# A decoder layer on one core: the products of two stages take PSUM banks of several kinds in turn

## The chip, the core and the metric

The kernel runs on one core of a Trainium2 chip. The core has a matrix engine (TensorE, PE in the profile), two engines that work element by element (VectorE, DVE; ScalarE, ACT), a small general one (GpSimd, POOL) and a queue that starts transfers (SyncE, SP). A product of TensorE lands in PSUM, which this kernel uses as eight banks of 128 x 512 float32; VectorE or ScalarE reads it from there. The metric is the device time of one execution in microseconds (us).

## The reference, cut to what matters

One layer for 1024 tokens of width 1024, in float32:

```python
u = rms_norm(h, norm1_g)
aq, ak, av, hq, hf, hi, hg = split(u @ w_in)
attn = rms_norm(dilated_attention(aq, ak, av), attn_norm_g)       # 8 heads
rec = rms_norm(hgrn2_mixer(hq, hf, hi, lb), hgrn_norm_g) * silu(hg)  # 4 heads, chunks of 64
h = h + concat([attn, rec]) @ w_out
u = rms_norm(h, norm2_g)
gate, val = split(u @ w_up)                                       # 2 x 2816 columns
h = h + (gelu(causal_conv3(gate)) * val) @ w_down
return rms_norm(h, final_norm_g)
```

In `hgrn2_mixer` a state of 128 x 128 per head is carried from chunk to chunk; inside a chunk there are products of queries with keys, of the masked result with the values, and of the queries with the state.

## The kernel before

All data lie transposed, features on the 128 partitions and tokens in two halves (`hf`) of 512 columns. Each float32 product is made as three passes: an operand is split into a rounded part (`hi`) and the rest (`lo`), and a block of 512 columns costs `hi*hi`, `hi*lo` and `lo*hi` for each block of 128 rows (`three`, L491 to L493; in the up stage `prod`, L1239 to L1241). The weights come by DMA into a ring of five slots, where ScalarE makes `whi` (L89) and VectorE `wlo` (L91).

The program runs in stages, one after the other on TensorE:

1. Token products, the first query/key blocks, then attention with the remaining query/key blocks between its parts (to 266 us in the profile).
2. The recurrent stage (266 to 389 us). The generator `dense` yields dense products: four blocks for pairs of head projections (`hg_block`, which is `pair_block`: seven products each, combined by additions, in the manner of Strassen), then `plain_block` with four plain products (`phf`, `phq`). Between them `play` sets in the steps of the recurrence, eight chains `recur(h, hf)`, by a table of times: transposes of the keys (`psK`), scores (`psA`), state updates (`psU`), outputs (`psO`), a transpose of the outputs (`psT`). Two sums for the attention's norm (`ass`) come in too.
3. The out-projection (389 to 493 us): `out_block`, 32 products `po`, with the rest of the recurrence and the norm of the first half between them (`norm2(0)`).
4. The up stage begins with six plain products for columns 0 and 1 (`p0g`, `p0v`, `p1g` ...), with `norm2(1)` between the first two: its sum `ss2_1` is two TensorE passes over the parts `acchi` and `acclo` of the accumulated squares. Then 20 blocks of seven products each (`up`), from another pool of eight PSUM banks.
5. The down stage and the final norm.

TensorE's order is the program's own. On the other engines a scheduler sets the order.

Up to the end of stage 4's plain products, `bank(tag, name)` hands out PSUM. There are four kinds (tags) of bank, `mm`, `o`, `t` and `s`, two banks each, and each kind hands out its two in turn: a tile has to wait until the tile two before it in its own kind has been read. The dense products and the out-projection take `mm` alone, the recurrence `s` (`psA`, `psU`), `t` (`psK`, `psT`, also `ass` and `ss2`) and `o` (`psO`). For the last ten products of the out-projection the kinds are already `mm`, `mm`, `s`, `o` in turn, before and after the change.

Of the seven products of a `pair_block`, most are read by one VectorE instruction; the product 5 is read by two (L528 and L529), with other VectorE work between them.

Of the kernel before, what the change touches and what calls it, by code (L numbers as in the profile page):

```python
# [251 lines left out]
def hybrid_kernel(ctx: ExitStack, tc: tile.TileContext, xT, w_qk, w_tok, w_hg, w_out, w_up,  # L252
# [134 lines left out]
    def bank(tag, name):  # L387
        return ps1.tile([P, H2], F32, tag=tag, name=name, bufs=2)
# [13 lines left out]
    def mtile(name):  # L402
        return at.tile([P, H2], F32, tag="m", name=name, bufs=3)
# [51 lines left out]
    def rms1_row(hf):  # L455
        ss = bank("s", f"ss{hf}")
        PE.matmul(ss, ones, sums[hf], start=True, stop=True)
        rstd(R1[:, halves[hf]], xp.tile([P, H2], F32, tag="sq", name=f"rt{hf}", bufs=2), ss, 1.0 / DM)
# [39 lines left out]
    def product(ps, key, i):  # L498

        x, op = TERMS[i]  # L500
        hi, lo = ring.get((key, x))
        bh, bl = opn[op]
        for c in range(KS):
            s = slice(c * P, (c + 1) * P)
            three(ps, (hi[:, s], lo[:, s]), (bh[:, c], bl[:, c]), c == 0, c == KS - 1)
            if c == KS - 1:
                ring.done((key, x))
            yield 0.65

    def pair_block(key, tiles, evac):  # L510

        def step(i):
            blocks.append(i)
            ps = bank("mm", f"w{len(blocks)}")
            yield from product(ps, key, i)
            return ps

        c1 = tiles(0, 0)
        ACT.copy(c1, (yield from step(1)))
        u = tiles(0, 1)  # L520
        DVE.tensor_sub(u, c1, (yield from step(6)))
        DVE.tensor_add(c1, (yield from step(2)), c1)
        evac(0, 0, c1)
        w = tiles(1, 0)
        DVE.tensor_add(w, (yield from step(7)), u)
        x = tiles(1, 1)
        p5 = yield from step(5)
        DVE.tensor_sub(x, p5, w)  # L528
        DVE.tensor_sub(u, u, p5)  # L529
        evac(1, 1, x)  # L530
        DVE.tensor_sub(w, (yield from step(4)), w)
        evac(1, 0, w)
        DVE.tensor_add(u, (yield from step(3)), u)
        evac(0, 1, u)

    blocks = []

    def tok_step(key, c, banks, order):

# [13 lines left out]
    def plain_product(ps, key, hf):  # L553

        for c in range(NCT):
            hi, lo = ring.get((key, c // KS))
            s = slice(c % KS * P, (c % KS + 1) * P)
            bh, bl = opn[OPS1[2 * hf + c // KS]]
            three(ps, (hi[:, s], lo[:, s]), (bh[:, c % KS], bl[:, c % KS]), c == 0, c == NCT - 1)
            if hf and c % KS == KS - 1:  # L560
                ring.done((key, c // KS))
            yield 0.65
# [62 lines left out]
    def run(g):  # L625
        for _ in g:
            pass
# [9 lines left out]
    def qk_evac(p):  # L637
        def evac(m, hf, src):
            if p not in qk:
                qk[p] = [at.tile([P, SEQ], F32, tag=x, name=f"{x}{p}", bufs=2) for x in ("qp", "kp")]  # L640
            t = halves[hf]
            nat = [x.rearrange("p (b l r) -> p b l r", l=32, r=4) for x in (src, R1[:, t])]
            DVE.tensor_mul(qk[p][m][:, t].rearrange("p (b r l) -> p b l r", l=32, r=4), *nat)
        return evac

    def qk_block(p):
        return pair_block(("qk", p), lambda m, hf: mtile(f"u{p}_{m}{hf}"), qk_evac(p))

    FAR, NEAR = 192, 256
    mask = at.tile([P, FAR + NEAR], F32, name="mask")  # L650
    first = qk_block(0)
    for _ in range(KS + 1):
        next(first)
    for hf in range(2):
        rms1_row(hf)
    run(first)
    fill.add(*[qk_block(p) for p in range(1, 4)])
    fill.run(3.9)
    xp_cm.__exit__(None, None, None)
# [164 lines left out]
    with pool("hg", "right") as hg:  # L824
# [8 lines left out]
        def tile_of(kind, h, hf):  # L833
            tag, bufs = {"hf": ("A", 4), "hq": ("E", 5), "hg": ("GH"[h // 2], 4)}[kind]
            return ht(tag, f"{tag}{h}_{hf}", bufs)
# [35 lines left out]
        def hg_block(pair):  # L871

            def evac(m, hf, src):
                DVE.tensor_mul(src, src, R1[:, halves[hf]])
                OUT[pair[m][0]](pair[m][1], hf, src)

            return pair_block(pair, lambda m, hf: tile_of(*pair[m], hf), evac)

        def plain_block(pair):

            for hf in range(2):
                for kind, h in pair:
                    ps = bank("mm", f"p{kind}{h}_{hf}")
                    yield from plain_product(ps, (kind, h), hf)
                    x = tile_of(kind, h, hf)
                    DVE.tensor_mul(x, ps, R1[:, halves[hf]])
                    OUT[kind](h, hf, x)

        def restore():

            for c in range(KS):
                hi, lo = (y[:, c] for y in opn["T4"])
                x = ring.raw(xT[c, :, halves[1]])
                ACT.mul(hi, x, col(V_G1 + c))
                DVE.scalar_tensor_tensor(lo, x, col(V_G1 + c), f32(hi), op0=ALU.mult, op1=ALU.subtract)

        def dense():

            for pair in HG[1:-1]:
                yield from hg_block(pair)  # L900
            restore()
            yield from plain_block(HG[-1])
# [159 lines left out]

        fill.add(dense())
        N = 3.5 * (len(HG) - 2) + 4.0
        steps = []
# [67 lines left out]
            if part:  # L1135
                square(hf, d)

        out_banks = cycle(("mm",))

        def square(hf, d):  # L1140
            t = halves[hf]
# [30 lines left out]
    def norm2(hf):  # L1172
        t = halves[hf]
        ss = bank("t", f"ss2_{hf}")
        sum_parts(ss, accs[hf])
        yield
        if hf:
            y, tt = otile("cv", "r2y_1", 2), otile("w", "r2t_1", 1)
        else:
            y, tt = (n2p.tile([P, H2], F32, name=f"r2{x}_0") for x in "yt")  # L1180
        R = rstd_part(y, tt, ss, 1.0 / DM)
        for c in range(NCT):
            if hf:
                uf = uf1[c] = atile(f"uf2_1_{c}")
            else:
                uf = n2p.tile([P, H2], F32, tag="uf", name=f"uf2_0_{c}", bufs=2)
            DVE.scalar_tensor_tensor(uf, h_[:, c, t], col(V_G2 + c), R, op0=ALU.mult, op1=ALU.mult)
            hi, lo = u2[hf][c]
            ACT.copy(hi, uf)
            DVE.tensor_sub(lo, uf, f32(hi))  # L1190
        yield
# [9 lines left out]
    out_banks = cycle(("mm", "mm", "s", "o"))  # L1201
# [43 lines left out]
    def plain(f, which, hf, last, ps):  # L1245
        for i, x in enumerate(("a11", "a12") if which == "g" else ("a21", "a22")):
            prod(ps, (x, f), u2[hf][i * KS : (i + 1) * KS], i == 0, i == 1, last)
# [70 lines left out]


    n2 = norm2(1)  # L1320
    p0 = {"g": bank("mm", "p0g"), "v": bank("mm", "p0v")}
    plain(0, "g", 0, False, p0["g"])
    next(n2)
    next(n2)
# [33 lines left out]
    with pool("ps2", "left", space=PSUM) as ps2:  # L1358

        def bank2(name):  # L1360
            return ps2.tile([P, H2], F32, tag="u", name=name, bufs=8)
# [159 lines left out]
        for x, y in STAGES:  # L1521
# [10 lines left out]
            ps = [bank2(f"d{x}_{d}") for d in range(KS)]  # L1532
# [107 lines left out]
```

## Time and profile before

| | us |
|---|---|
| median of 3 runs | 1146.88 |
| lowest and highest run | 1146.65, 1148.97 |
| the profiled execution | 1147.14 |
| its span, first to last instruction | 1145.4 |

The profile is of one execution. A row of its timeline gives the start in us, the duration, the engine, the line of the kernel, the operation, and output <- inputs by the program's names with their numbers left out; what stands in brackets is how long the engine was idle before it and what released it. A matmul's duration overlaps with that of the next one: what counts for TensorE is the distance from start to start. The view by windows gives the busy time of each engine in a stretch of time, and in the column PEclk the granted clock of TensorE as a share of full speed.

### The profile page before, as it was taken

How to read it: one execution, taken by the hardware profiler on the slowest of the kernel's cores; microseconds unless marked ns; L12 is line 12 of the kernel's file. 1: busy time of each engine (PE TensorE's matmuls, PEld its weight loads, DVE VectorE, ACT ScalarE, POOL GpSimd, SP SyncE). 2: the span in 40 equal slices, each digit the busy share in tenths (PEclk: the TensorE clock that was granted, in tenths of full speed). 3: DMA queues.
4: the chain of work that ended last, by engine and by line, in shares of the span. 5: the costliest groups of instructions: out<-in, count | busy, mean ns of one | idle time of the engine just before them, and what ended most of it. 6: DMA issues, size and time to landing. Idle time of an engine off the chain costs nothing.

```text
span 1145.4 us, 17931 instructions
## 1 busy us (share of the span) xinstructions
PE 1131.1 (99%) x6416; PEld 928.9 (81%) x6416; DVE 959.7 (84%) x1748; ACT 586.6 (51%) x1177; POOL 88.2 (8%) x107
## 2 busy tenths in 40 slices
PE   9999999999999999999999999999999999999996
PEld 7887777778888888878788888888888888888885
DVE  7676877778999975889999989888988789857987
ACT  6544445465787875555433434343434354444553
POOL 5200233330000002000000000000000000000000
PEclk9999999999999999999999999999999999999998
DMA  7135221224313543221233223322332376335432
GB/s 250 59 99 152 64 76 58 84 75 161 116 59 102 174 129 101 84 65 46 74 111 117 87 100 129 111 82 95 126 111 83 117 267 230 116 98 175 157 120 74
DMA packets 98633, 129.84 MB, mean 113 GB/s; under 512 B 25008, under 2 KB 44240, under 8 KB 98544
## 3 DMA queue, kind: packets, MB, share of 16 engines
q1 hardware_dynamic: 83984, 103.77, 29.2%
q10 hardware_dynamic: 14560, 24.94, 5.8%
q8 instruction: 50, 0.82, 0.3%
q14 instruction: 39, 0.32, 0.1%
HBM read 97.58 MB, written 31.09 MB: 112 GB/s over the span
## 4 chain that ended last, share of the span: by engine, by line
PE 90%; DVE 7%; issue 1%; ACT 1%; DMA 1%; ACTq 0%; DVEq 0%; SPq 0%
PE p L1241 11%; PE p L1239 11%; PE p L1240 11%; PE w L491 5%; PE w L493 5%; PE w L492 5%; PE ds L1540 3%; PE ds L1538 3%; PE ds L1539 3%; PE da L1540 2%; PE da L1538 2%; PE da L1539 2%; PE po L491 2%; PE po L493 2%; PE po L492 2%; PE S L711 2%
## 5 line engine op out<-in xcount | busy, mean ns | idle before, releaser
L89 ACT CAST whi<-raww 128x512 fp32r<-128x512 f32 x257 | 157.3, 617 | 217.9 <-PE p L1240 74.0
L91 DVE TENSOR_TENSOR wlo<-raww,whi 128x512 fp32r<-128x512 f32 x258 | 179.8, 699 | 29.9 <-ACT whi L89 27.9
L89 ACT CAST whi<-r 128x512 fp32r<-128x512 f32 x70 | 43.6, 623 | 83.8 <-PE ds L1539 49.3
L91 DVE TENSOR_TENSOR wlo<-r,whi 128x512 fp32r<-128x512 f32 x70 | 47.9, 685 | 19.3 <-ACT whi L89 18.7
L1538 PE MATMUL ds<-fhi,whi 128*128 128x512 f32 x160 | 62.3, 389 | 0.0
L1540 PE MATMUL ds<-fhi,wlo 128*128 128x512 f32 x160 | 62.2, 389 | 0.0
L1239 PE MATMUL p<-b1h,whi 128*128 128x512 f32 x160 | 62.2, 389 | 0.0
L1240 PE MATMUL p<-b1l,whi 128*128 128x512 f32 x160 | 62.2, 389 | 0.0
L1241 PE MATMUL p<-b1h,wlo 128*128 128x512 f32 x160 | 62.2, 389 | 0.0
L1539 PE MATMUL ds<-flo,whi 128*128 128x512 f32 x160 | 62.2, 389 | 0.0
L724 POOL TENSOR_SCALAR P<-P,st 128x128 f32<-128x128 f32 (+7 forms) x64 | 46.5, 734 | 99.0 <-DVE st L723 91.9
L1512 POOL TENSOR_TENSOR facc<-facc,sqf 128x256 f32<-128x256 f32 x2 | 1.5, 740 | 674.0 <-ACT sqf L1511 674.0
L91 DVE TENSOR_TENSOR flo<-rawf,fhi 128x512 fp32r<-128x512 f32 x70 | 47.9, 684 | 3.2 <-ACT fhi L89 3.2
L89 ACT CAST fhi<-rawf 128x512 fp32r<-128x512 f32 x70 | 43.2, 617 | 13.4 <-PE p L1241 5.0
L722 ACT ACTIVATE P<-P,st 128x128 f32<-128x128 f32 (+7 forms) x64 | 35.7, 559 | 27.5 <-DVE st L720 27.5
L1268 ACT ACTIVATE cv<-cv 128x512 f32<-128x512 f32 x44 | 27.8, 632 | 41.0 <-DVE cv L1261 41.0
L1261 DVE SCALAR_TENSOR_TENSOR cv<-g,vec,cv 128x511 f32<-128x511 f32 (+2 forms) x92 | 44.6, 490 | 3.6 <-ACT cv L1258 3.3
L1538 PE MATMUL da<-fhi,whi 128*128 128x512 f32 x120 | 46.7, 389 | 0.0
L1539 PE MATMUL da<-flo,whi 128*128 128x512 f32 x120 | 46.7, 389 | 0.0
L1540 PE MATMUL da<-fhi,wlo 128*128 128x512 f32 x120 | 46.7, 389 | 0.0
L720 DVE CUSTOM_DVE_ANT_0 P<-S,mask 128x128 f32<-128x128 f32 (+7 forms) x64 | 28.9, 487 | 10.0 <-PE S L713 7.5
L1539 PEld LDWEIGHTS ds<-flo,whi 128*128 128x128 f32 x160 | 30.0, 188 | 6.3
(622 smaller groups left out, 3405.4 us busy)
## 6 DMA issues: line engine op xcount, KB each, us to landing
raww<-in_w_up_dram SPq DMA_DIRECT2D x88, 256.0 KB, 2.9
rawf<-spT SPq DMA_DIRECT2D x40, 256.0 KB, 2.8
r<-in_w_down_dram SPq DMA_DIRECT2D x40, 256.0 KB, 3.4
spB<-a ACTq DMA_DIRECT2D x30, 256.0 KB, 2.2
spT<-t ACTq DMA_DIRECT2D x30, 256.0 KB, 2.2
rawf<-spB SPq DMA_DIRECT2D x30, 256.0 KB, 2.7
raww<-in_w_out_dram SPq DMA_DIRECT2D x28, 256.0 KB, 2.8
raww<-in_w_hg_dram SPq DMA_DIRECT2D x24, 256.0 KB, 2.6
```

What stands on the lines that cost most here:

```text
L89: self.pin(self.high(hi[:, :w], raw))
L91: self.pin(low.tensor_sub(lo[:, :w], raw, f32(hi[:, :w])))
L491: PE.matmul(ps, a[0], b[0], start=start, stop=False)
L492: PE.matmul(ps, a[0], b[1], start=False, stop=False)
L493: PE.matmul(ps, a[1], b[0], start=False, stop=stop)
L724: POOL.tensor_scalar(Pt[:, :n], Pt[:, :n], st[:, 3:4], 1.0, op0=ALU.mult, op1=ALU.mult)
L1239: PE.matmul(ps, hi[:, s], bhi, start=(start and n == 0), stop=False)
L1240: PE.matmul(ps, hi[:, s], blo, start=False, stop=False)
L1241: PE.matmul(ps, lo[:, s], bhi, start=False, stop=(stop and n == len(rhs) - 1))
L1538: PE.matmul(ps[d], hi[:, s], ahi, start=(k == 0), stop=False)
L1539: PE.matmul(ps[d], hi[:, s], alo, start=False, stop=False)
L1540: PE.matmul(ps[d], lo[:, s], ahi, start=False, stop=(k == NPAIR - 1))
```

## The change

Four places in the code decide the kind of bank. The dense products of the recurrent stage take `mm`, `o`, `t` in turn. The first 22 products of the out-projection take `mm`, `mm`, `o` in turn. The first product of the up stage, `p0g`, takes `t`. The earlier query/key blocks go through the same new code and still take `mm`.

```diff
@@ pair_block
         def step(i):
             blocks.append(i)
-            ps = bank("mm", f"w{len(blocks)}")
+            ps = bank(next(block_banks[0]), f"w{len(blocks)}")
             yield from product(ps, key, i)
             return ps
...
-    blocks = []
+    blocks, block_banks = [], [cycle(("mm",))]
...
     first = qk_block(0)
+    block_banks[0] = cycle(('mm',))
...
     run(first)
+    block_banks[0] = cycle(("mm",))
...
@@ plain_block
-                    ps = bank("mm", f"p{kind}{h}_{hf}")
+                    ps = bank(next(block_banks[0]), f"p{kind}{h}_{hf}")
...
+        block_banks[0] = cycle(('mm', 'o', 't'))
         fill.add(dense())
...
-        out_banks = cycle(("mm",))
+        out_banks = cycle(('mm', 'mm', 'o'))
...
     n2 = norm2(1)
-    p0 = {"g": bank("mm", "p0g"), "v": bank("mm", "p0v")}
+    p0 = {"g": bank("t", "p0g"), "v": bank("mm", "p0v")}
```

No instruction is added, removed or moved on TensorE, ScalarE, GpSimd or SyncE. On VectorE two pairs of neighbours change places, in the first dense block. What changes is where TensorE waits, and for whom. In the rows below, `waits` names the engine whose counter a row waits for; the rows are in the program's order, with the tiles' numbers.

On TensorE, in the first dense block, at the seventh product (`w42`; `w41` is the sixth, `w40` the product 5 that two VectorE instructions read). Before:

```order
L493 MATMUL w41_3434<-T4h_95,wlo56_3323 128x512
L491 MATMUL w42_3453<-B22h_101,whi57_3342 128x512 [waits DVE_49,Activation_49]
L492 MATMUL w42_3453<-B22l_102,whi57_3342 128x512
L493 MATMUL w42_3453<-B22h_101,wlo57_3343 128x512
L491 MATMUL w42_3453<-B22h_101,whi57_3342 128x512
```

and now:

```order
L493 MATMUL w41_3434<-T4h_95,wlo56_3323 128x512
L491 MATMUL w42_3453<-B22h_101,whi57_3342 128x512 [waits Activation_49]
L492 MATMUL w42_3453<-B22l_102,whi57_3342 128x512
L493 MATMUL w42_3453<-B22h_101,wlo57_3343 128x512 [waits DVE_49]
L491 MATMUL w42_3453<-B22h_101,whi57_3342 128x512
```

The first pass no longer waits for VectorE (before: for L529, the second reader of `w40`). The wait for VectorE that now stands at the third pass is for its operand `wlo57`, which the old wait had covered.

On TensorE, in the second dense block, at the sixth product `w48` (`w46`, two before it, is read by L525). Before:

```order
L493 MATMUL w47_3628<-T1h_97,wlo62_3467 128x512
L491 MATMUL w48_3656<-T4h_95,whi63_3503 128x512 [waits DVE_49]
L492 MATMUL w48_3656<-T4l_96,whi63_3503 128x512
L493 MATMUL w48_3656<-T4h_95,wlo63_3504 128x512
L1026 MATMUL psO0_0_3666<-iv0_0_3397,AT_3306 128x128 x2
```

and now:

```order
L493 MATMUL w47_3628<-T1h_97,wlo62_3467 128x512
L491 MATMUL w48_3656<-T4h_95,whi63_3503 128x512 [waits DVE_49,Activation_49]
L492 MATMUL w48_3656<-T4l_96,whi63_3503 128x512
L493 MATMUL w48_3656<-T4h_95,wlo63_3504 128x512 [waits DVE_49]
L1028 MATMUL psO0_0_3666<-iv0_0_3397,AT_3306 128x128 [waits Activation_49]
```

`w48` now waits for the reader of `w42` (L533), six products back, and the recurrence's `psO` waits for the reader of a dense product that had its bank, `w43` (L519 on ScalarE).

On TensorE, from the out-projection's last product to the up stage's first. Before:

```order
L492 MATMUL po1_1_7_5616<-rec1l_5336,whi110_5516 128x512
L493 MATMUL po1_1_7_5616<-rec1h_5335,wlo110_5517 128x512
L1239 MATMUL p0g_5745<-b1h0_5349,whi111_5539 128x512 [waits DVE_49,Activation_49]
L1240 MATMUL p0g_5745<-b1l0_5350,whi111_5539 128x512
L1241 MATMUL p0g_5745<-b1h0_5349,wlo111_5540 128x512
```

and now:

```order
L492 MATMUL po1_1_7_5616<-rec1l_5336,whi110_5516 128x512
L493 MATMUL po1_1_7_5616<-rec1h_5335,wlo110_5517 128x512
L1242 MATMUL p0g_5745<-b1h0_5349,whi111_5539 128x512 [waits Activation_49]
L1243 MATMUL p0g_5745<-b1l0_5350,whi111_5539 128x512
L1244 MATMUL p0g_5745<-b1h0_5349,wlo111_5540 128x512
```

The wait for VectorE's addition L1134 on the bank of `po1_1_6` is gone from `p0g`.

## The prediction

> **What bounds the kernel now.** I read the engines' totals first, then the waits of TensorE, then windows over the touched stages, and last the timeline around each wait there.
>
> ```profile
> PE 1131.1 (99%) x6416; PEld 928.9 (81%) x6416; DVE 959.7 (84%) x1748; ACT 586.6 (51%) x1177; POOL 88.2 (8%) x107
> ```
>
> TensorE is busy for 99% of the span. Its order and its work stay as they are, so the change can only win idle time of TensorE, or add some. The view of waits lists all of it that has a releaser (engine, line waited for: total, times, longest):
>
> ```profile
> PE v L545 <- ACT B11h L435: 1.2, 1, 1.2
> PE warm L419 <- DVE eps L280: 1.1, 1, 1.1
> PE w L491 <- DVE G L529: 0.8, 1, 0.8
> PE p0g L1239 <- DVE h L1134: 0.8, 1, 0.8
> PE w L491 <- DVE u L522: 0.5, 1, 0.5
> PE p L1241 <- DVE wlo L91: 0.3, 1, 0.3
> ```
>
> The first two are from the program's start, and `u L522` is from the token products, which keep their banks. Two lines lie where the change is: `G L529` and `h L1134`. The last one, on a weight, lies behind them. So what is to be won is small from the outset. The windows (busy time of PE, PEld, DVE, ACT, POOL; then the granted clock, DMA share, GB/s) tell who could stand in the way:
>
> ```profile
> 300.00:400.00 100.00, 100.00 (x555) 82.85 (x555) 97.58 (x180) 86.11 (x219) 3.67 (x3) 1.00 0.35 108
> 471.00:496.00 25.00, 24.23 (x107) 19.79 (x106) 24.87 (x41) 14.57 (x25) 0.00 (x0) 1.00 0.30 95
> 502.00:556.00 54.00, 53.61 (x235) 43.56 (x234) 53.32 (x90) 29.98 (x50) 0.00 (x0) 1.00 0.12 40
> ```
>
> From 300 to 400 us TensorE never stops, though VectorE has only 2.42 us of slack in the 100. Before the seam of the two stages (471 to 496) VectorE is full: 0.13 us idle of 25. After it, it is nearly full again.
>
> **First place: the bank of `w42`.** The timeline:
>
> ```profile
> 282.54 0.39 PE L492 MATMUL w<-T4l,whi 128*128 128x512 f32 x1
> 282.76 0.39 PE L493 MATMUL w<-T4h,wlo 128*128 128x512 f32 x1
> 283.17 0.68 DVE L529 TENSOR_TENSOR G<-G,w 128x512 f32<-128x512 f32 x1
> 284.00 0.47 PE L491 MATMUL w<-B22h,whi 128*128 128x512 f32 x1 [0.85 <-DVE G L529]
> 284.30 0.39 PE L492 MATMUL w<-B22l,whi 128*128 128x512 f32 x1
> ```
>
> An unhindered pass starts 0.23 us after the one before it (282.76 minus 282.54, rounded up; the longer rows of such starts come to 0.2275). Here 1.24 us lie between starts, 1.01 too many, and the first pass after the pause takes 0.30 in place of 0.23, another 0.07: 1.08 us. L529 is the second reader of `w40` and ends at 283.85; TensorE starts 0.15 us later. With three kinds in turn `w42` takes another bank, and its wait for L529 goes. Its operand `wlo` had been made blocks before. I take the whole 1.08. If something else that the trace hides behind this wait were late too, it could be less, down to 0.
>
> **Second place: the bank of `w48`.**
>
> ```profile
> 302.43 0.68 DVE L525 TENSOR_TENSOR E<-w,A 128x512 f32<-128x512 f32 x1
> 302.81 0.39 PE L493 MATMUL w<-T1h,wlo 128*128 128x512 f32 x1
> 303.17 0.50 PE L491 MATMUL w<-T4h,whi 128*128 128x512 f32 x1
> 303.50 0.40 PE L492 MATMUL w<-T4l,whi 128*128 128x512 f32 x1
> ```
>
> L525 ends at 303.11 and the pass starts at 303.17. The gap is 0.36, thus 0.13 too long, and the next start is 0.33 away, 0.10 too long: 0.23 us. It too goes, since `w48` now waits for a reader six products back.
>
> **Third place: the bank of `p0g`.**
>
> ```profile
> 492.73 0.39 PE L493 MATMUL po<-rec1h,wlo 128*128 128x512 f32 x1
> 493.05 0.69 DVE L1134 TENSOR_TENSOR h<-po,h 128x512 f32<-128x512 f32 x1
> 493.89 0.47 PE L1239 MATMUL p0g<-b1h,whi 128*128 128x512 f32 x1 [0.77 <-DVE h L1134]
> 494.19 0.39 PE L1240 MATMUL p0g<-b1l,whi 128*128 128x512 f32 x1
> ```
>
> The gap is 1.16, so 0.93 too many, and 0.07 for the first pass: 1.00 us. The `t` bank that `p0g` takes held the last `psT` of the recurrence, whose reader ends at 464.80, long before:
>
> ```profile
> 464.05 0.75 DVE L1043 SCALAR_TENSOR_TENSOR H<-psT,vec,H 128x512 f32<-128x512 f32 x1
> ```
>
> So no reader is in the way there. The three sum to 1.08 + 0.23 + 1.00 = 2.31 us.
>
> **What is late next.** The second half's norm is summed by two passes between the first products of the up stage, and the second of them needs `acclo`, which VectorE makes:
>
> ```profile
> 470.97 0.39 PE L493 MATMUL po<-attn1h,wlo 128*128 128x512 f32 x1
> 471.39 0.69 DVE L1134 TENSOR_TENSOR h<-po,xr 128x512 f32<-128x512 f32 x1
> 498.22 0.69 DVE L366 TENSOR_TENSOR acclo<-sq,acchi 128x512 fp32r<-128x512 f32 x1 [0.69 <-ACT acchi L365]
> 499.45 0.39 PE L371 MATMUL ss<-acchi,ones 128*128 128x512 f32 x1
> 499.68 0.39 PE L371 MATMUL ss<-acclo,ones 128*128 128x512 f32 x1
> 500.13 0.69 ACT L355 ACTIVATE r2t<-ss,eps 128x512 f32<-128x512 f32 x1
> ```
>
> VectorE's addition at 471.39 starts where TensorE's product ends (470.97 + 0.39 = 471.36), and from there to 496 it runs back to back. It therefore comes earlier by the gains of the first two places, 1.31 us, but not by the third: freeing `p0g` makes nothing on VectorE earlier. `acclo` is ready at 498.91 - 1.31 = 497.60; with the 0.15 us of the first place it lets TensorE start at 497.75. TensorE would be there at 499.68 - 2.31 = 497.37. So 0.38 us go back into a new wait, and what is left is 1.93 us. In general the gain is the smaller of 2.31 and 0.62 + x, where x is how much earlier VectorE comes (0.62 is 499.68 minus 498.91 minus 0.15).
>
> Behind the sum stand ScalarE's root at 500.13, VectorE's scaling and the rest of the plain products. VectorE is nearly full there (53.32 of 54), and TensorE has two pauses on a weight's `wlo`:
>
> ```profile
> 552.66 0.50 PE L1241 MATMUL p<-b22h,wlo 128*128 128x512 f32 x1 [0.27 <-DVE wlo L91]
> ```
>
> As both engines move by the same 1.93 us behind the sum, this pause stays as it is.
>
> **The waits that are new.** Dense products now share banks with the recurrence's transposes, outputs and sums, so those wait for readers of dense products, and the reverse. A new wait costs nothing while its reader has ended before TensorE arrives, and otherwise at most what it lacks; the nearest price of a wait that does strike is the first place's 1.08, so each lies between 0 and 1.08. It can't gain, since a wait makes nothing earlier. The nearest cases:
>
> ```profile
> 317.82 0.74 DVE L1043 SCALAR_TENSOR_TENSOR G<-psT,vec,G 128x512 f32<-128x512 f32 x1
> 322.06 1.02 PE L916 MATMUL ass<-asq,ones 128*128 128x512 f32 x2
> 350.80 0.69 DVE L358 SCALAR_TENSOR_TENSOR asq<-ass,asq 128x512 f32<-128x512 f32 x1 [0.64 <-ACT asq L357]
> 355.55 0.60 PE L987 MATMUL psK<-ident,B 128*128 128x128 f32 x4
> ```
>
> The attention's sum `ass` starts 322.06 - 318.56 = 3.50 us after the reader that its tile's bank would wait for, and `psK` 355.55 - 351.49 = 4.06 us after its own. If VectorE did not move with TensorE, 1.31 less would remain, 2.19: still enough. I take 0.
>
> The out-projection's two kinds in turn bring its next reader from two products back to three at the least, but no pause stands there between 390 and 492 to be won: 0. `p0v` keeps `mm`: its bank is read before 494, and it starts six microseconds later: 0. The two swapped pairs on VectorE cost the same 0.7 us each in either order: 0. No DMA is added, and no queue is passed.
>
> **The sum.** The profiled execution took 1147.14 us (span 1145.4), 0.26 above the median. 1147.14 - 1.93 = 1145.21; against the median, 1146.88 - 1.93 = 1144.95, so 1145.0. 0.2% of it, 2.29 us, is about what a measurement of this kernel can tell from no change: faster means below 1144.59, slower above 1149.17. My forecast is a true gain just inside that bound.
>
> **Rivals.**
>
> *The sum pass does not wait.* If VectorE comes earlier than I think, by 1.69 or more, all of 2.31 stays: 1144.57, at the edge of faster. For it speaks that VectorE idles 0.69 us on ScalarE's `acchi` right ahead of `acclo`; against it that its queue from 471.39 hangs on TensorE's product and has 0.13 us idle, so that it can hardly come more than 1.44 earlier.
>
> *VectorE takes the early gain back.* With 97.58 of 100 us busy, it may not follow the 1.31 us, and a wait for a weight or a bank comes back elsewhere before 471. Then x is 0, `p0g` starts early, the sum waits for the old time of `acclo`, and 0.62 is left: 1146.3. Against it: 2.42 us idle in that window are more than the 1.31 it has to win. With nothing left at all it would be 1146.9.
>
> *The other side: `ass` and the transposes behind dense readers.* A dense product in a `t` bank has one to two VectorE readers, and the recurrence's next tile in `t` now waits for them. With VectorE's queue full, a reader may come late. It begins to cost from 3.50 us of lateness at `ass`, and one us for each further one. To end above 1149.17 it must eat the gain and 2.29 more, that is 3.50 + 1.93 + 2.29 = 7.72 us late, eleven VectorE instructions of 0.69. Just beyond that the time is 1149.5. Against it stands that the stage now runs without a pause from 303.50 on.
>
> *The clock.* The rows above show a granted clock of 1.00 in all touched windows. In the last stretch, where TensorE idles more, it is lower:
>
> ```profile
> 266.00:494.00 228.00, 226.38 (x1207) 187.62 (x1204) 197.82 (x354) 164.07 (x397) 11.68 (x10) 1.00 0.38 117
> 1100.00:1145.00 45.00, 35.91 (x203) 30.90 (x201) 33.86 (x71) 16.95 (x37) 1.48 (x2) 0.92 0.35 117
> ```
>
> If taking banks in turn cost the touched stretch 0.92 of the clock, its 228 us would become 248, and the time 1166.7. Against it: TensorE is busy for 226.38 of the 228, and the change shortens its pauses. [...]
>
> **How the numbers follow.** My forecast of 1145.0 has 0.53; its own range is 1144.4 to 1145.5, and about 0.09 of it falls below 1144.59, since the three terms are read from rows of 0.01 us but the runs shown differ by more (1146.65 to 1148.97). The sum pass without a wait has 0.16, the early gain taken back 0.23, the transposes behind dense readers 0.06, the clock 0.02. Faster: 0.16 + 0.09 = 0.25. Within 0.2%: 0.53 - 0.09 + 0.23 = 0.67. Slower: 0.08. The range from 1144.0 to 1147.0 takes in the first three, and at its upper end no gain.
>
> **What the profile after would show.** The waits of TensorE without `G L529` and `h L1134`; the passes of `w42` and `p0g` 0.23 us after their predecessors; a new wait of 0.2 to 0.4 us of `ss` for `acclo`; the pause on `wlo` near 551 still there; VectorE's additions after 303 earlier by 1.3 us; and a span of 1143.5. I am wrong if the two waits are gone and another stands between 303 and 471 (the second rival), if `ss` waits for longer than 0.4 us, or if PEclk falls below 1.00 between 266 and 494.

## The result, and the profile after

| | before | after |
|---|---|---|
| median of 22 runs, us | 1146.99 | 1145.17 |
| lowest, highest, us | 1146.65, 1148.97 | 1144.59, 1146.80 |
| the profiled execution, its span, us | 1147.14, 1145.4 | 1146.50, 1144.7 |

The ratio after to before is 0.9983, with an interval of 0.9977 to 0.9989: the change saves 1.95 us (1.3 to 2.6). The forecast was 1145.0.

The two profiled executions differ by 0.64 us only, because executions of both kernels fall into two groups 1.5 to 1.8 us apart, and the profiled one of before is in the lower group (the runs within 1 us of a kernel's fastest), that of after in the higher. The medians of the lower groups are 1146.93 (15 of the 22 runs) and 1144.92 (12 of 22), 2.01 us apart. Small terms are told apart below by the lower groups of kernels that were measured side by side, or by TensorE's start times in one trace against those in another.

The groups part at the very start, on TensorE, in the timeline of before (first two rows) and of after:

```profile
8.20 0.40 PE L545 MATMUL v<-whi,B11h 128*128 128x512 f32 x1
8.43 0.39 PE L546 MATMUL v<-wlo,B11h 128*128 128x512 f32 x1
```

```profile
8.23 0.63 PE L545 MATMUL v<-whi,B11h 128*128 128x512 f32 x1
8.66 0.63 PE L546 MATMUL v<-wlo,B11h 128*128 128x512 f32 x1
```

Two neighbouring passes at the same time: 0.23 us apart in the one, 0.43 us in the other, and so until about 10.4 us, when after is 1.7 us behind before with the same pass. It enters the touched stretch 1.5 us late, for a reason that the change has no part in: runs of both kernels have such starts.

The waits of TensorE, after:

```profile
PE v L545 <- ACT B11h L435: 1.1, 1, 1.1
PE warm L419 <- DVE eps L280: 1.1, 1, 1.1
PE w L491 <- DVE u L522: 0.3, 1, 0.3
PE ss L371 <- DVE acclo L366: 0.2, 1, 0.2
PE p L1244 <- DVE wlo L91: 0.2, 1, 0.2
```

`G L529` and `h L1134` are gone, and the wait of `ss` for `acclo` is new. The windows:

```profile
300.00:400.00 100.00, 100.00 (x553) 83.14 (x553) 97.93 (x182) 86.81 (x221) 3.67 (x3) 1.00 0.36 107
471.00:496.00 25.00, 25.00 (x112) 20.71 (x111) 24.87 (x41) 14.56 (x25) 0.00 (x0) 1.00 0.30 95
266.00:494.00 228.00, 228.00 (x1242) 190.14 (x1239) 198.83 (x357) 164.96 (x399) 11.69 (x10) 1.00 0.38 118
```

From 266 to 494 us TensorE is now busy for all of the 228 us (before: 226.38). The three places in the timeline of after, first `w42`:

```profile
284.31 0.39 PE L493 MATMUL w<-T4h,wlo 128*128 128x512 f32 x1
284.53 0.39 PE L491 MATMUL w<-B22h,whi 128*128 128x512 f32 x1
284.76 0.39 PE L492 MATMUL w<-B22l,whi 128*128 128x512 f32 x1
```

then `w48`:

```profile
303.24 0.39 PE L493 MATMUL w<-T1h,wlo 128*128 128x512 f32 x1
303.47 0.39 PE L491 MATMUL w<-T4h,whi 128*128 128x512 f32 x1
303.69 0.39 PE L492 MATMUL w<-T4l,whi 128*128 128x512 f32 x1
```

and the seam, with the new wait:

```profile
492.89 0.39 PE L493 MATMUL po<-rec1h,wlo 128*128 128x512 f32 x1
493.12 0.39 PE L1242 MATMUL p0g<-b1h,whi 128*128 128x512 f32 x1
493.35 0.39 PE L1243 MATMUL p0g<-b1l,whi 128*128 128x512 f32 x1
...
498.38 0.69 DVE L366 TENSOR_TENSOR acclo<-sq,acchi 128x512 fp32r<-128x512 f32 x1 [0.69 <-ACT acchi L365]
498.56 0.39 PE L371 MATMUL ss<-acchi,ones 128*128 128x512 f32 x1
...
499.12 0.50 PE L371 MATMUL ss<-acclo,ones 128*128 128x512 f32 x1 [0.17 <-DVE acclo L366]
499.47 0.40 PE L1242 MATMUL p0v<-b1h,whi 128*128 128x512 f32 x1
```

Each place is now 0.23 us from pass to pass. The start of one and the same pass, after minus before, gives each term apart from the late start: the last pass of `w41` 284.31 - 282.76 = 1.55, the second of `w42` 284.76 - 284.30 = 0.46; so 1.09 won. Around `w48` from 303.24 - 302.81 = 0.43 to 303.69 - 303.50 = 0.19; 0.24 won. At the seam from 492.89 - 492.73 = 0.16 to 493.35 - 494.19 = -0.84; 1.00 won. At the sum, the pass behind `acclo` starts 0.56 us after the one ahead of it, and `p0v` another 0.35 later: 0.33 + 0.12 = 0.45 given back.

### The profile page after: what moved, and what is told of

Read it like the earlier page. It is cut to its first block, busy times and chain, and to the rows that moved or that the text cites. A ratio compares the mean times of both kernels' runs of the same rounds, so it can differ in the third digit from the quotient of the medians.

```text
span 1144.7 us, 17933 instructions
## 1 busy us (share of the span) xinstructions
PE 1132.4 (99%) x6416; PEld 930.4 (81%) x6416; DVE 958.5 (84%) x1748; ACT 587.0 (51%) x1177; POOL 88.7 (8%) x107
## 4 chain that ended last, share of the span: by engine, by line
PE 91%; DVE 7%; ACT 1%; issue 1%; DMA 1%; ACTq 0%; DVEq 0%; SPq 0%
PE p L1244 11%; PE p L1242 11%; PE p L1243 11%; PE w L491 5%; PE w L493 5%; PE w L492 5%; PE ds L1543 3%; PE ds L1541 3%; PE ds L1542 3%; PE da L1543 2%; PE da L1541 2%; PE da L1542 2%; PE po L491 2%; PE po L493 2%; PE po L492 2%; PE S L713 2%
## 5 line engine op out<-in xcount | busy, mean ns | idle before, releaser
L91 DVE TENSOR_TENSOR wlo<-r,whi 128x512 fp32r<-128x512 f32 x70 | 47.9, 685 | 19.8 <-ACT whi L89 18.9
```

The costliest lines, as they stand in the source:

```text
L91: self.pin(low.tensor_sub(lo[:, :w], raw, f32(hi[:, :w])))
```

## The experiments

Four kernels undo or do parts of the change. `e1`, only the dense products:

```diff
-        out_banks = cycle(('mm', 'mm', 'o'))
+        out_banks = cycle(("mm",))
-    p0 = {"g": bank("t", "p0g"), "v": bank("mm", "p0v")}
+    p0 = {"g": bank("mm", "p0g"), "v": bank("mm", "p0v")}
```

> Only the dense products of the recurrent stage take three kinds; the out-projection and p0g take mm as before. Theory (the prediction's terms add up one by one): the first two places go, 1.08 + 0.23 = 1.31 us below the kernel before; the wait for L529 is gone, p0g still waits 0.77 us for L1134, the sum's second pass does not wait, and behind 494 TensorE is earlier by the same 1.31. Rival (VectorE takes the early gain back): a new wait between 303 and 471, and 0 to 0.3 us below the kernel before.

`e2`, only `p0g`:

```diff
-        block_banks[0] = cycle(('mm', 'o', 't'))
+        block_banks[0] = cycle(('mm',))
-        out_banks = cycle(('mm', 'mm', 'o'))
+        out_banks = cycle(("mm",))
```

> Only p0g takes the kind t; all other products take mm. Theory (gain = the smaller of the waits removed and 0.62 + x, here with x = 0): p0g starts 0.93 us earlier, the sum's second pass then waits some 0.38 us for acclo, and 0.62 us are left. Rival (the sum pass is not bound by VectorE): no wait there, and the whole 1.00 us.

`e3`, only the out-projection:

```diff
-        block_banks[0] = cycle(('mm', 'o', 't'))
+        block_banks[0] = cycle(('mm',))
-    p0 = {"g": bank("t", "p0g"), "v": bank("mm", "p0v")}
+    p0 = {"g": bank("mm", "p0g"), "v": bank("mm", "p0v")}
```

> Only the first 22 products of the out-projection take mm, mm, o. Theory: no wait stood there, so 0 us, with the waits for L529 and L1134 as before. Rival (a third bank lets VectorE's additions run ahead, so that L1134 comes earlier at p0g): up to 1.00 us, and a shorter wait of p0g.

`e4`, all but the out-projection:

```diff
-        out_banks = cycle(('mm', 'mm', 'o'))
+        out_banks = cycle(("mm",))
```

> The dense products and p0g as in the changed kernel, the out-projection on mm alone as before. Theory: the same as the changed kernel, 1.9 us below the kernel before, with the sum's second pass waiting 0.2 to 0.4 us for acclo. Rival (the out-projection's kinds carry a part): the waits of the out-projection for L1134 come back once TensorE is early, and the gain is nearer to 1.3 us.

Measured (the kernel before beside them: 1146.82, lower group 1146.77; "less than before" is between lower groups):

| | median, us | ratio, interval | lower group, us | less than before | forecast |
|---|---|---|---|---|---|
| `e1` dense | 1145.44 | 0.9989, 0.9981 to 0.9998 | 1145.36 | 1.41 | 1.31 |
| `e2` p0g | 1147.62 | 0.9998, 0.9989 to 1.0007 | 1146.18 | 0.59 | 0.62 |
| `e3` out-projection | 1146.76 | 1.0, 0.9991 to 1.0009 | 1146.72 | 0.05 | 0 |
| `e4` dense and p0g | 1144.79 | 0.9982, 0.9973 to 0.9991 | 1144.78 | 1.99 | 1.93 |

`e1` and `e4` lie clear of no change in their intervals; `e2` does not, since six of its eleven runs were of the higher group, and what it gains is read from the lower group and the trace. The waits of `e1` and of `e2` that stand in the touched stretch:

```profile
PE p0g L1242 <- DVE h L1137: 0.8, 1, 0.8
```

```profile
PE w L491 <- ACT whi L89: 0.9, 1, 0.9
PE ss L371 <- DVE acclo L366: 0.2, 1, 0.2
```

The first line of `e2` is the wait of `w42`, which `e2` keeps: the view names another releaser, but the pass starts at 285.51, 0.14 us after L529 has ended, as before. `e1` keeps the wait of `p0g` and gains no other; its `acclo` is made at 496.70 (before 498.22; 0.13 of the 1.52 were won ahead of the touched stretch), and its sum does not wait. `e2` has the wait of the sum in place of that of `p0g`. In its timeline:

```profile
499.74 0.69 DVE L366 TENSOR_TENSOR acclo<-sq,acchi 128x512 fp32r<-128x512 f32 x1 [0.69 <-ACT acchi L365]
...
499.91 0.40 PE L371 MATMUL ss<-acchi,ones 128*128 128x512 f32 x1
500.48 0.50 PE L371 MATMUL ss<-acclo,ones 128*128 128x512 f32 x1 [0.18 <-DVE acclo L366]
```

This execution started late: the last products of the out-projection and `acclo` both stand 1.52 us after their times of before, so `acclo` did not move against the out-projection, as x = 0 in the prediction says. TensorE won 0.93 and 0.07 at `p0g` and lost 0.40 at the sum. The rivals fall: VectorE did follow the early gain (`e1`), the sum does bind (`e2`), and the out-projection's kinds carry nothing (`e3`, `e4`).

`e8` takes the third kind from the dense products:

```diff
-        block_banks[0] = cycle(('mm', 'o', 't'))
+        block_banks[0] = cycle(('mm', 'o'))
```

> The changed kernel, but the dense products take two kinds, mm and o, in turn instead of three. Theory: w42 and w48 then wait for readers of products four back or of psO, which ended long before, so both waits are gone as with three kinds, and the time is that of the changed kernel within 0.2 us. Rival (the third kind is needed, since psO now comes more often between): a part of the 1.37 us comes back as waits on o.

Measured: 1145.14 (0.9981, 0.9972 to 0.9990). From 122 us to the out-projection's first pass its TensorE wins 1.37 us on before, as does the changed kernel. Two kinds do it; the third is not needed.

`e7` makes them share one kind with the recurrence:

```diff
-        block_banks[0] = cycle(('mm', 'o', 't'))
+        block_banks[0] = cycle(('t',))
```

> The changed kernel, but the dense products of the recurrent stage take the kind t alone, which they share with psK, psT and ass. Theory (a wait strikes where the reader is the one of the product just before): ten psK, psT and ass stand between dense products; each makes the next dense product wait for the reader of the one before, about 1.0 us each as at the first and third place, and the waits of the kernel before on the product two back stay, 1.3 us: some 11 us above the changed kernel. Rival (sharing a kind with the recurrence costs nothing by itself, VectorE reads early enough): within 1.5 us of the changed kernel.

Measured: 1164.28 in one run, 19.1 us above the changed kernel's median, more than the 11 expected; by the start times in the two traces it loses 18.9. The larger waits of its TensorE:

```profile
PE psK L989 <- DVE A L533: 2.6, 1, 2.6
PE ass L918 <- DVE A L522: 2.1, 1, 2.1
PE psT L1043 <- ACT A L519: 2.1, 1, 2.1
...
PE phf L491 <- DVE G L1045: 1.4, 1, 1.4
```

I had priced only the dense product that follows a recurrence's tile. The worst waits are the other way round: `psK`, `psT` and `ass` stand in the middle of a dense product and wait for the reader of the one before (the first `psT` comes three passes into a product, so that this reader had 0.7 us in which to come). So the mechanism of the rival on the other side is real; with two or three kinds in turn the waits of TensorE (`e8`, the changed kernel) list none of these.

More is lost than the pauses alone. Three of them (2.59, 2.08 and 2.11 us) fall within 19 us, and behind the third the granted clock shows 0.50 over two us and 0.68 over the next two. The windows, then two neighbouring passes:

```profile
328.00:330.00 2.00, 0.24 (x1) 0.24 (x2) 2.00 (x4) 0.59 (x2) 0.00 (x0) 0.97 0.00 0
330.00:332.00 2.00, 2.00 (x4) 0.87 (x4) 1.33 (x3) 0.20 (x1) 0.00 (x0) 0.50 0.00 0
332.00:334.00 2.00, 2.00 (x8) 1.57 (x7) 0.00 (x0) 2.00 (x5) 0.00 (x0) 0.68 0.00 0
```

```profile
332.41 0.63 PE L493 MATMUL w<-T3h,wlo 128*128 128x512 f32 x1
332.84 0.60 PE L491 MATMUL w<-T3h,whi 128*128 128x512 f32 x1
```

The passes are 0.43 us apart in place of 0.23, and from `ass` at 329.76 to the pass at 333.26 `e7` takes 3.50 us, the changed kernel 1.78 for the same (322.23 to 324.01). The ten pauses of `e7` between 266 and 408 us come to 14.2 us; with 1.7 for the slow passes and some 0.2 behind each pause, as at the first place, that is some 18 of the 18.9 us, an estimate. In the kernel before and the changed one the clock is 1.00 from 266 to 494 us, in `e1` from 266 to 390, in `e2`, `e3` and `e4` from 300 to 390. That the pauses lowered it is thus the likely reading, from one run.

`e5` puts the second half's sum three passes later, into `p0v`:

```diff
-    next(n2)
-    next(n2)
-    plain(0, "v", 0, False, p0["v"])
+    plain(0, "v", 0, False, p0["v"], lambda: (next(n2), next(n2)))   # called behind its first three passes
```

> The changed kernel, but the two passes of the second half's sum stand behind the first three passes of p0v instead of ahead of them. Theory (behind the sum VectorE sets the end): the sum's second pass no longer waits, which is 0.40 us won for TensorE there, but it runs some 0.3 us later than in the changed kernel, VectorE's chain starts as much later, and the pauses on wlo near 551 grow by about 0.7; the time is that of the changed kernel or up to 0.3 us more. Rival (TensorE bounds all the way): the pauses on wlo stay, and the time is 0.4 us below the changed kernel.

Measured: 1146.35 (0.9987, 0.9977 to 0.9996), only 4 of the 11 runs in the lower group, at 1144.93. That is 1.73 below the kernel before beside it (lower group 1146.66), where the changed kernel was 2.01 below: 0.28 us are lost, at the upper end of what was expected. The traces give the same 0.28. The sum no longer waits, which wins 0.47 us on the changed kernel, and more than that is lost again. Where it is lost is not the pause that I named (idle for 0.18 us at 550.29; 0.15 in the changed kernel), but this one, in the timeline, which costs 0.68:

```profile
512.88 0.50 PE L1243 MATMUL p1g<-b22l,whi 128*128 128x512 f32 x1 [0.50 <-DVE b22l L1193]
```

`b22l` is made by VectorE from the norm whose sum had been put off. That VectorE's chain sets the end there was right, and its place wrong.

`e6` carries the change's own idea to the one wait on a bank that is left, `u L522` in the first query/key block:

```diff
     first = qk_block(0)
-    block_banks[0] = cycle(('mm',))
+    block_banks[0] = cycle(('mm', 't'))
```

> The changed kernel, and the first query/key block of the token stage takes mm and t in turn, so that the product that waited for u L522 finds another bank. Theory: that wait goes as the others did; the pause was 0.68 us and 0.10 in the pass behind it (0.59 together where the start was slower), VectorE comes earlier by the same, and 0.6 to 0.8 us below the changed kernel are left at the end, 2.6 to 2.8 below the kernel before. Rival (VectorE or a weight of the same product is late too, or VectorE's full queue in attention takes it back): another wait stands near 109 or before 266, and 0 to 0.2 us.

Measured: 1144.02 (0.9972, 0.9960 to 0.9983), lower group 1144.01, 2.65 below before beside it (1146.66), 0.64 more than the changed kernel's 2.01. The waits of its TensorE, all of them:

```profile
PE warm L419 <- DVE eps L280: 1.1, 1, 1.1
PE v L545 <- ACT B11h L435: 1.0, 1, 1.0
PE ss L371 <- DVE acclo L366: 0.2, 1, 0.2
```

`u L522` is gone and nothing has come for it. Between the token sums at 99 us and the first scores at 122 its TensorE wins 0.83 us on before, and still has it at the end.

`e9` adds a second buffer for the squares of the out-projection's second half:

```diff
-            sq = None if d == 0 else otile("w", f"sq2_{hf}_{d}", 1)
+            sq = None if d == 0 else otile(*(("g", f"sq2_{hf}_{d}", 2) if hf and d % 2 else ("w", f"sq2_{hf}_{d}", 1)))
```

> The kernel of the experiment before that also frees the first query/key block, and the squares of the out-projection's second half alternate between two buffers in place of one. Theory (the last square waits on ScalarE for its one buffer, 1.17 us idle until VectorE's addition to acc, and this sets acclo, not VectorE's queue alone): VectorE's last sum of squares comes 0.19 us earlier (then behind its split of alow), acclo too, the sum's second pass loses 0.2 instead of 0.40, and up to 0.2 us are won at the end. Rival (VectorE's full queue alone sets acclo): acclo and the wait stay as they are.

Measured: 1145.29 (0.9977, 0.9968 to 0.9985), 5 of 12 runs in the lower group, at 1144.11 against 1144.01 for `e6`, 2.61 and 2.65 below before: the times do not show a gain. The trace shows the step. The row of before that raised the question is ScalarE's last square, and below it the same one in `e9`:

```profile
496.18 0.63 ACT L1147 ACTIVATE sq<-h 128x512 f32<-128x512 f32 x1 [1.17 <-DVE acc L1149]
```

```profile
495.11 0.63 ACT L1150 ACTIVATE sq<-h 128x512 f32<-128x512 f32 x1 [0.51 <-DVE h L1137]
```

It waited for its only buffer, which VectorE's addition to `acc` had to free, and now waits for its own operand. `acclo` comes 0.19 us earlier against the out-projection, the sum's loss falls from 0.40 to 0.20, and between 122 us and the end `e9` wins 0.16 us more than `e6`. So by the trace this buffer, and not VectorE's queue alone, set half of what was given back.

`e10` is `e6` with more warming products ahead of the first real one:

```diff
-    busy(9)
+    busy(12)
```

> The same kernel with twelve warming products ahead of the first product in place of nine, so that TensorE's pause there shrinks from about 1.0 us to nothing. Theory (in some executions TensorE starts its products at 0.43 us a pass because of this pause): all executions start at 0.23, and none is 1.5 to 1.8 us above the others. Rival (it depends on something that is not in the program, so the pause has no part in it): such executions go on, a third to a half of all.

Measured: 1144.14 (0.9966, 0.9953 to 0.9979); all five runs lie within 0.4 us. But TensorE's pause ahead of its first product was 0.94 us in the profiled execution, so the reason that I gave was not put to the test. `e11` has all of it: `e9` with the twelve warming products.

> All edits that helped in one kernel: the changed kernel, two kinds for the first query/key block, two buffers for the squares, twelve warming products. Theory (the terms add up, and the longer warming keeps the slow first passes away): no execution 1.5 us or more above the others, the pauses for u L522 and most of that for acclo gone, some 3.0 us below the kernel before. Rival (the five even executions with twelve warming products were luck): a third to a half of the executions are again 1.5 to 1.8 us above the others.

Measured: 1143.88 (0.9966, 0.9952 to 0.9979), five runs within 0.6 us. Of the 26 runs of the kernel before that stand beside `e10` and `e11`, 12 are in its higher group, and none of the ten with twelve warming products stands above its fellows. Luck is not ruled out: with nine warming products 7 of 12 runs of `e9` are in the higher group, but only one of six of `e6`. The one wait of TensorE that the view still lists for `e11`:

```profile
PE warm L419 <- DVE eps L280: 1.1, 1, 1.1
```

This is the best version, faster than both kernels: 0.34% below the kernel before by the ratio (0.17% for the change alone), in which the missing late starts have a part, and 2.8 us in the lower groups (1146.70 and 1143.88).

## Why the prediction was right, point by point

- *The first two places*, 1.08 + 0.23: 1.09 and 0.24 in the trace, 1.41 in the times of `e1`.
- *The third place*, 1.00: 1.00 in the trace.
- *What is late next*: the wait of `ss` for `acclo` came where it was put. Forecast 0.38, measured 0.45 in the changed kernel and 0.40 in `e2`: the sum's second pass is 0.33 late, and the pass behind it another 0.12, which I had left out here, though it is in the three places (0.07 to 0.10). VectorE's additions were to come earlier by 1.3 us after 303. They do, but not at once: L525 of the second place comes 0.79 earlier against TensorE's start (303.19 after, 302.43 before, less 1.55), and only from about 360 on it is 1.38, as at 471 (471.56 and 471.39). The formula of 0.62 + x held at both values of x that were tried: 0.59 in the times at x = 0 (`e2`), 1.99 at x = 1.31 (`e4`, formula 1.93). What I said of its reason was half of it: VectorE's full queue (24.87 of 25 us busy from 471 to 496) keeps `acclo` where it is, but the single buffer of the squares set its last 0.2 us (`e9`).
- *The new waits*, 0: none shows; and `e7` shows what they cost when the margin is gone, up to 2.59 us for one. That each would lie below 1.08 us was wrong as a bound, though nothing hung on it here.
- *The out-projection's kinds*, 0: 0.05 us in `e3`, within its interval.
- *The pause on `wlo`* was to stay at 0.27 us idle. It is 0.15 here:

```profile
552.08 0.50 PE L1244 MATMUL p<-b22h,wlo 128*128 128x512 f32 x1 [0.15 <-DVE wlo L91]
```

  From `p0v` (499.47 - 499.91 = -0.44) to the rest of the program (-0.63) the changed kernel wins another 0.19 us, and `e1`, which has no wait at the sum, 0.17. This is hardly the change's doing: `e3`, which has won nothing ahead of it, wins 0.14 in the same stretch, and its pass at this place comes 0.53 us after the one before it (551.59 to 552.12), against 0.65 before (552.01 to 552.66) and 0.54 in the changed kernel. Why the pause differs between executions stays open.
- *The sum of it*: 1.55 + 0.44 = 1.99 us from the touched stretch to `p0v` in the trace, 2.18 to the end with the 0.19 just told, 2.01 in the lower groups, 1.95 by the ratio; forecast 1.93. That the median, 1145.17, lies so close to 1145.0 is in part chance: 10 of the 22 runs after had the slow start, 7 of the 22 before. The span that I named, 1143.5, came out as 1144.7 because of the slow first passes of that execution.
- *The rivals*: the sum pass waits; the early gain is not taken back; the clock stays at 1.00 in all touched windows of the changed kernel. Taking banks in turn removed pauses of TensorE, and no pass in the rows of after is longer for it than 0.23 us from start to start, behind a wait apart. That pauses between products cost clock is the likely reading of `e7` alone: one kind for all brought pauses of 2 us and more, and the clock fell to 0.50 over two us.

## What to carry to other kernels

When one engine is busy for 99% of the span, list its waits by releaser, measure each as the distance between starts less the normal distance (the pass behind the wait included), and then ask of each gain what else the next step needs: a wait on a bank that is removed shifts only what hangs on this engine, and the next operand that another engine makes late gives part of it back (here 0.45 us of 2.33). Banks that other kinds leave free were a cheap cure here for a wait on a reader two products back (1.41 us in `e1`), but not all sharing is: two kinds in turn did as well as three, and one kind shared with short tiles cost 19 us, some 1.7 of them in slow passes at the lower granted clock. When two profiles of nearly the same kernel are compared, subtract start times pass by pass; the spans alone would have shown a third of this change.

## What the runs showed of the hardware

The first passes of TensorE run at 0.43 us each up to about 10.4 us in the traces of after, `e2` and `e9`, whose profiled executions are of the higher groups, and at 0.23 in those of before, `e3`, `e4` and `e6`, which are of the lower ones. Between after and before this makes 1.74 us at the start (the same pass at 10.63 and 8.89); the wait for `u L522`, 0.3 us in after and 0.5 in before, then absorbs some 0.2 of it. The column PEclk shows 1.00 in both (windows from 6 to 10 us, before and after):

```profile
6.00:10.00 4.00, 3.62 (x16) 3.04 (x17) 3.45 (x5) 3.77 (x8) 0.00 (x0) 1.00 1.01 352
```

```profile
6.00:10.00 4.00, 3.64 (x10) 2.96 (x11) 3.45 (x5) 3.62 (x7) 0.00 (x0) 1.00 1.06 380
```

16 passes against 10 at the same granted clock. So at the start it is seen in the distance between starts, and not in that column. In the middle of the program the column does tell: the two passes of `e7` 0.43 us apart (332.41 and 332.84) lie in two us at a granted clock of 0.68, behind two us at 0.50. What brings the slow start is not shown; the two groups of times are in the runs of most kernels. With twelve warming products none of ten executions was of the higher group. The length of the pause ahead of the first product does not decide it: `e6` and `e9` paused alike there (0.97 us), and `e6` started fast, `e9` slowly; `e4` paused 1.48 us and started fast. Whether the three more products did anything stays open.
